# A two-layer DeltaNet and attention kernel: query heads' squared sums as four packed products, T joins spaced in the planner, and a new order in the scan's pool

## The chip, the cores and the metric

The kernel runs on one core of one Trainium2 chip. The metric is the device time of one execution in microseconds (us), taken as the median of several runs; lower is better. The core has five engines that matter here: TensorE (PE) multiplies matrices, VectorE (DVE), ScalarE (ACT) and GpSimd (POOL) work elementwise, and SyncE (SP) issues most of the DMA transfers. Each engine runs its instructions in the order in which they were written for it.

## The reference, cut to what matters

The input is 512 latent tokens and 256 context tokens of width 1024. Layer 0 is a bidirectional gated DeltaNet with 8 query/key heads and 16 value heads of width 128; layer 1 is attention; a final RMSNorm gives the output. Both layers read the tokens through an adaLN-modulated norm. The part around the change is this, from layer 0:

```python
p = u @ w_in                                           # 1024 -> q, k, v, z and gates
qkv = jax.nn.silu(centred_dwconv(p[..., :DN_CONV_DIM], conv_w))
q, k, v = jnp.split(qkv, [DN_KEY_DIM, 2 * DN_KEY_DIM], axis=-1)
q = jnp.repeat(l2_norm(q.reshape(b, l, DN_QK_HEADS, DN_HEAD_K)), rep, axis=2)
...
t_inv = lax.linalg.triangular_solve(eye + a, ...)      # per chunk of 64 tokens, per head
...
def step(s, xs):                                       # the scan over chunks
    v_new = u_i - jnp.einsum('bhcd,bhde->bhce', w_i, s)
    o = jnp.einsum('bhcd,bhde->bhce', qd_i, s) + jnp.einsum('bhcs,bhse->bhce', qk_i, v_new)
    s = s * gl_i[..., None, None] + jnp.einsum('bhcd,bhce->bhde', kd_i, v_new)
```

`l2_norm` needs, for each token and query head, the sum over 128 channels of the squared query. The kernel keeps queries unnormalised and applies this sum late, as a factor on the DeltaNet output (`rq`).

## The kernel before, in words

The core works through these stages: an opening (0 to about 44 us) that loads the tokens and forms the modulated, transposed input `uh` + `ul` (a high and a low part, so that fp32 accuracy comes from three fast products); the key heads (to about 134 us); the **planned stage** (134 to 541 us); the scan over chunks (541 to about 720 us); the output projection of layer 0 (to about 900 us); and layer 1.

In the planned stage PE forms 40 heads in the order of the string `order` (L898): 8 query (q), 16 value (v) and 16 gate (z) heads. One head is two `gemm_part` pieces (L919), the 512 latent columns and the 256 context columns, each of 24 products (8 slices of depth, three products each). Before a head's product its weights are split, by `w_high` on ACT and `w_low` on DVE or POOL (L914). After it come the convolution (`taps`), tanh and silu on ACT and DVE. A value head is then turned to token rows by PE (`head_turned`) and stored in DRAM.

A query head's squares (`head_squared`, ACT) lie with channels on the 128 partitions and the 768 tokens along the row. `head_summed` (L972) sums them over the partitions with PE: twelve products, one per chunk of 64 tokens, each with 64 columns of squares as the stationary operand and a column of ones as the moving one. `sums_copied` (L983) has ACT copy the 6 result columns into `rq`. One Newton series on DVE makes the roots of all of `rq` near the end of the stage (L1434).

Beside the heads, the stage makes the matrices T (the triangular solves) for six pairs of chunks, t = 0 to 5, in three solve pairs. Row loads and `decay` (L732, ACT), `m_prod` (L776, DVE) and turns build the input L of a pair, for which POOL runs a long chain of small column steps (`solve_steps`, L798). Then each t is **joined**: `j_turn` (L822, DVE), `j_first` (L830, PE, 64 products of 32 x 32), a negation on ACT, `j_second` (L854, PE, 64 products of 32 x 32), and copies on ACT into `Tt`, which `j_stored` (L851) writes to DRAM. Pair 2 (t = 4 and 5) is solved last. Each of the 64 products stands as two instructions in the trace with a weight load each, so that a join is 128 matmul records and as many weight loads.

The order of all this on the engines is written by a planner in the kernel's own Python. Every step is a `Piece` (L1037) with an engine, an assumed cost, a due time, the pieces that it comes after, and the buffers that it takes. `written_out` (L1110) repeatedly takes the piece that could start first by its model, and among equals the one that is due first, and so writes every engine's instruction order, SP's included. `margin` (L1055) adds a reserve of 3.0 us to PE pieces other than the `gemm_part` ones, which it knows by their cost.

The scan has 12 steps of 4 groups each. Step 0 needs no queries; its operands are loaded ahead by planned pieces (`first_matrices`, `first_values`). From step 1 on `load_step` (L1516) has SP issue the loads of keys (`ck`), values (`cv`), T (`cT`), QK (`cQK`), queries (`cq`) and turned keys (`ckt`). Their tiles come from the pool `ch` (L1450), which is laid over the planned stage's pool `tp`: both end at the same address, and inside a pool tiles lie in the order in which they are first asked for. A load therefore waits until the old tile under its target has been read for the last time. In the layout before, the query tile of step 1 lies over `U_5`, the last T's transposed solve, which `j_second` of t = 5 reads.

Of the kernel before, what the change touches and what calls it, by code (L numbers as in the profile page):

```python
# [17 lines left out]
P = 128  # L18
# [68 lines left out]
def backbone(tc, a, out):  # L87
# [147 lines left out]
    two = ap_.tile([P, 64], F32, tag="two", name="two", bufs=1)  # L235
    room = {}
# [8 lines left out]
    def opened():  # L245
# [10 lines left out]
        V.memset(ones, 1.0)  # L256
        V.memset(square, 1.0)
# [661 lines left out]
    def gemm_part(n, i):  # L919
        c, h = heads[n]  # L920
        wh, wl = split_w_[n]
        c0, m = COLS[i]
        ps = banks[n, i] = pa.tile([P, 512], F32, tag="g", name=f"g{m}_{c}{h}", bufs=4)
        for k in range(KT):
            for n_, (w, u) in enumerate(((wh, uh), (wh, ul), (wl, uh))):
                T.matmul(ps[:, :m], w[:, k], u[:, k, c0:c0 + m], start=k == 0 and n_ == 0, stop=k == KT - 1 and n_ == 2)  # L926
# [45 lines left out]
    def head_summed(n):  # L972
        ps = turns[n] = pa.tile([P, 512], F32, tag="tr", name=f"ss_q{heads[n][1]}")
        sq = sums.pop(n)
        for t in range(NT):
            for hf in range(2):
                c0 = t * P + hf * 64
                T.matmul(ps[hf * 64:hf * 64 + 64, t:t + 1], sq[:, c0:c0 + 64], ones, start=True, stop=True)
# [4 lines left out]
    def sums_copied(n):  # L983
        S.copy(rq[:, :, heads[n][1]], turns.pop(n)[:, 0:NT])
# [52 lines left out]
    class Piece:  # L1037
        def __init__(self, engine, cost, due, fn, *args, after=(), takes=(), holds=(), lands=0.0, since=0.0, slack=None, behind=(), port=0, sent=0.0, far=0.0):
# [3 lines left out]
            self.fn, self.end, self.takes = lambda: fn(*args), None, list(takes)  # L1042
            self.users = {x: [] for x in self.takes}
            for x, owner in holds:
                owner.users[x].append(self)
            pieces.append(self)

# [7 lines left out]
    def margin(x):  # L1055
# [4 lines left out]
        return MARGIN.get(x.engine, 0.0) if x.engine != "PE" else 0.0 if x.cost in (5.48, 2.96) else MARGIN["PE"]  # L1060
# [49 lines left out]
    def written_out():  # L1110

        left = list(pieces)
        while left:
            best = None
            for x in left:
# [12 lines left out]

    SLOT = 8.8
# [195 lines left out]
    for n, (c, h) in enumerate(heads):  # L1325
# [5 lines left out]
        g = []  # L1331
        for i in range(2):
            g.append(Piece("PE", (5.48, 2.96)[i], t0, gemm_part, n, i, after=[wh, wl] + ([last["g", n - 1]] if n and not i else g), takes=["g"], holds=[("wh", wh)], lands=0.2))
# [3 lines left out]
        if c != "z":  # L1337
            for i in range(2):
                ce = Piece("ACT", (0.65, 0.45)[i], e + (-2.9, 0.2)[i], centre, n, i, after=[g[i]] + a_[:1], takes=["acc"] if i == 0 else (), holds=[("g", g[i])] + ([("acc", a_[0])] if i else []), lands=0.1)
# [1245 lines left out]
```

## Time and profile before

| What | Value |
|---|---|
| Median of 3 runs | 1142.55 us (1142.25 to 1142.96) |
| The profiled execution | 1143.75 us, of which its span on the core is 1141.8 us |
| PE busy | 1107.7 us (97% of the span) |
| DVE, ACT, POOL busy | 790.3, 747.1, 602.1 us |
| TensorE clock granted, mean | 0.994 of full speed |
| Data moved by DMA | 208.69 MB, 183 GB/s on average |

The profile's rows give, for one profiled execution, an engine, a line of the kernel (L978 is line 978), the operation, the tile written and the tiles read, and times from the start of the span. Rows of the timeline begin with the start and the length; a bracket at the end tells the idle time of that engine ahead of the row and what ended it ("issue" is a gap for which no awaited event shows). Rows of a window give a stretch and each engine's busy time in it, then the granted clock, the share of the 16 DMA engines and the GB/s.

### The profile page before, as it was taken

What the parts mean: (1) busy time and instruction counts of PE and PEld (TensorE: products, weight loads), DVE (VectorE), ACT (ScalarE), POOL (GpSimd) and SP (SyncE); (2) the same over time, 40 slices, a digit from 0 to 9 for tenths busy, and PEclk for the clock granted to TensorE, in tenths of its full rate; (3) what the DMA queues carried; (4) which work ended last, traced back from release to release, by engine and by line L of the source; (5) the groups of instructions that cost most, each with busy time, mean ns of one, the idle gap of its engine ahead of it and who ended that gap; (6) DMA issues with size and microseconds to landing.
All of it is one profiled execution on the core that took longest, in us unless ns stands there. A gap on an engine that the chain in (4) does not pass through costs nothing. (4 is left out here: it accounts for less than half of the span.)

```text
span 1141.8 us, 27230 instructions
## 1 busy us (share of the span) xinstructions
PE 1107.7 (97%) x10511; PEld 904.8 (79%) x10511; DVE 790.3 (69%) x1628; ACT 747.1 (65%) x1990; POOL 602.1 (53%) x525
## 2 busy tenths in 40 slices
PE   5999999999999999998999999999999999999997
PEld 3677788888888888887666666788877889999886
DVE  4785666688899978783788878445555477667647
ACT  4554554477787888755689888875776356666731
POOL 0564111339999999950585598656654354130820
PEclk8999999999999999999999999999999999999999
DMA  9589744765838886766988984685854112101323
GB/s 367 187 297 329 254 151 124 226 175 163 238 123 246 262 250 201 200 209 185 283 236 255 279 241 129 206 216 173 246 162 139 37 56 75 38 19 57 111 74 92
DMA packets 117106, 208.69 MB, mean 183 GB/s; under 512 B 12113, under 2 KB 76786, under 8 KB 111730
## 3 DMA queue, kind: packets, MB, share of 16 engines
q1 hardware_dynamic: 97058, 195.32, 55.4%
q10 hardware_dynamic: 19920, 11.64, 3.5%
q8 instruction: 83, 1.36, 0.5%
q14 instruction: 45, 0.37, 0.1%
HBM read 166.16 MB, written 40.67 MB: 181 GB/s over the span
## 5 line engine op out<-in xcount | busy, mean ns | idle before, releaser
L1750 PE MATMUL po<-woh,y 128*128 128x512 f32 x384 | 129.3, 401 | 0.0
L1688 POOL TENSOR_TENSOR wol<-wo,woh 128x1024 fp32r<-128x1024 f32 x32 | 77.3, 2415 | 54.4 <-ACT woh L1681 52.6
L810 POOL TENSOR_TENSOR X<-X,tmp 128x62 f32<-128x62 f32 (+15 forms) x93 | 101.3, 1089 | 7.3
L1576 POOL TENSOR_TENSOR S<-S,glb 128x512 f32<-128x512 f32 x80 | 81.8, 1044 | 36.6 <-PE ks L1567 36.2
L809 POOL TENSOR_TENSOR tmp<-L,X 128x62 f32<-128x62 f32 (+15 forms) x93 | 89.1, 958 | 6.7
L926 PE MATMUL g_z<-ul,wh_z 128*128 128x512 f32 (+1 forms) x256 | 87.0, 340 | 3.0 <-issue 3.0
L926 PE MATMUL g_z<-uh,wh_z 128*128 128x512 f32 (+1 forms) x256 | 88.5, 346 | 0.2 <-issue 0.2
L926 PE MATMUL g_v<-uh,wh_v 128*128 128x512 f32 (+1 forms) x256 | 88.0, 344 | 0.0
L941 DVE SCALAR_TENSOR_TENSOR acc_v<-g_v,cwv,acc_v 128x510 f32<-128x510 f32 (+3 forms) x128 | 77.7, 614 | 14.5 <-ACT acc_v L933 11.0
L926 PE MATMUL g_z<-uh,wl_z 128*128 128x512 f32 (+1 forms) x256 | 86.6, 338 | 0.0
L926 PE MATMUL g_v<-ul,wh_v 128*128 128x512 f32 (+1 forms) x256 | 86.1, 336 | 0.0
L926 PE MATMUL g_v<-uh,wl_v 128*128 128x512 f32 (+1 forms) x256 | 86.1, 336 | 0.0
L1750 PEld LDWEIGHTS po<-woh,y 128*128 128x128 f32 x384 | 72.2, 188 | 15.6 <-issue 0.3
L1750 PE MATMUL po<-wol,y 128*128 128x512 f32 x192 | 75.5, 393 | 0.0
L1716 DVE SCALAR_TENSOR_TENSOR pt<-pt,og,z 128x128 f32<-128x128 f32 x96 | 34.4, 358 | 32.7 <-PE pt L1707 30.4
L1644 DVE TENSOR_TENSOR S<-su,S 128x512 f32<-128x512 f32 x80 | 51.5, 686 | 7.5 <-PE su L1630 5.9
L555 POOL TENSOR_TENSOR kt<-kt,kss 128x768 f32<-128x768 f32 x8 | 11.6, 1472 | 85.6 <-DVE kss L183 57.1
L926 PEld LDWEIGHTS g_z<-ul,wh_z 128*128 128x128 f32 x256 | 49.0, 191 | 8.4 <-issue 3.7
L1567 PE MATMUL ks<-S,ck 128*64 128x256 f32 x352 | 55.2, 392 | 0.0
L1570 DVE SCALAR_TENSOR_TENSOR r<-ks,negV,cv 128x128 f32<-128x128 f32 x176 | 52.3, 343 | 1.7 <-PE ks L1567 0.7
L1567 PE MATMUL ks<-S,cq 128*64 128x256 f32 x352 | 53.0, 379 | 0.3 <-DMA cq<-q_d 0.3
L926 PEld LDWEIGHTS g_z<-uh,wl_z 128*128 128x128 f32 x256 | 48.9, 191 | 5.3
(469 smaller groups left out, 3343.4 us busy)
## 6 DMA issues: line engine op xcount, KB each, us to landing
aw<-in_ada_late SPq DMA_DIRECT2D x16, 1024.0 KB, 6.9
wo<-in_dn_w_out SPq DMA_DIRECT2D x32, 512.0 KB, 3.7
cv<-v_d SPq DMA_DIRECT2D x22, 512.0 KB, 8.9
aw<-in_ada_first SPq DMA_DIRECT2D x8, 1024.0 KB, 10.4
w_z<-in_dn_w_in SPq DMA_DIRECT2D x16, 512.0 KB, 4.0
w_v<-in_dn_w_in SPq DMA_DIRECT2D x16, 512.0 KB, 4.5
v_d<-vt ACTq DMA_DIRECT2D x16, 384.0 KB, 4.0
cT<-t_d SPq DMA_DIRECT2D x12, 512.0 KB, 7.4
```

The lines of the kernel that those rows point to most:

```text
L555: G.tensor_tensor(kt, kt, bcast(r[:, h % 2 * NT:(h % 2 + 1) * NT], 2, P), ALU.mult)
L809: G.tensor_tensor(tv, bcast(L[:, :, j + 1:, j], 3, j + 1), bcast(X[:, :, j, 0:j + 1], 2, n), ALU.mult)
L810: G.tensor_tensor(X[:, :, j + 1:, 0:j + 1], X[:, :, j + 1:, 0:j + 1], tv, ALU.subtract)
L926: T.matmul(ps[:, :m], w[:, k], u[:, k, c0:c0 + m], start=k == 0 and n_ == 0, stop=k == KT - 1 and n_ == 2)
L941: V.scalar_tensor_tensor(acc[:, c0 + lo:c0 + hi], ps[:, lo + j - 2:hi + j - 2], cwv[:, j, ct:ct + 1], acc[:, c0 + lo:c0 + hi], ALU.mult, A ...
L1567: T.matmul(ks[r0:r0 + 64, w], kq[w][:, hh, r0:r0 + 64], St[hh][:, d], start=True, stop=True)
L1570: V.scalar_tensor_tensor(r[:, 2 * j + i], ks[:, 0, i], negV[:, visit, t, h:h + 1], v[:, h], ALU.mult, ALU.add)
L1576: G.tensor_tensor(St[hh], St[hh], bcast(g_, 3, P), ALU.mult)
L1644: V.tensor_tensor(St[hh], sj, St[hh], ALU.add)
L1688: G.tensor_tensor(wl, raws.pop(n), halves[n][0], ALU.subtract)
L1716: V.scalar_tensor_tensor(pj, pj, og, raw(z, off, [[st_, 2], [1, 64]]), ALU.mult, ALU.mult)
L1750: T.matmul(acc[nh], y[i][:, j, :], ww[k][:, nh * 512:(nh + 1) * 512], start=h == 0 and x == 0, stop=h == VH - 1 and x == 2)
```

## The change

It has five parts.

1. **Squared sums.** `head_summed` now keeps a small selector as stationary operand (`pick`, zeros with one column of ones, of which 32 columns are taken so that the ones stand in column h) and streams the squares: four products of 192 tokens each, one to each group of 32 columns of the array, so that row h of each group of the result holds head h's sums. DVE collects the 8 heads into `qrows` (128 x 192). After the last head, `sums_turned` turns them with six products against the identity, and `sums_kept` copies them to `rq` with two ACT copies.
2. **Joins apart.** The planner remembers the end of the last `j_first` or `j_second` and lets the next one count as startable only 4.0 us after it (`SPACED`).
3. **Halved heads.** For the last three heads (n = 37, 38, 39, all z) each `gemm_part` becomes two pieces of 12 products, between which the planner may put other PE work.
4. **Three due times.** `m_prod` of t = 5 is due 373 us later, one of the query-side `decay` pieces of t = 3 is due 22 us later, and `w_low` of head 10 is due 23 us earlier.
5. **Scan pool.** The tiles of `ch` are asked for once in a fixed order ahead of the scan, and the two `r` buffers become two tags, the second at the end. All tiles between them lie 2 KB per partition lower than before; the query tile of step 1 no longer touches `U_5`.

```diff
+    pick = ap_.tile([P, 64], F32, tag="pick", name="pick", bufs=1)
+    qrows = ap_.tile([P, 192], F32, tag="qrows", name="qrows", bufs=1)
...
+        V.memset(pick, 0.0)
+        V.memset(pick[:, 32:33], 1.0)
...
-    def gemm_part(n, i):
+    def gemm_part(n, i, half=None):
...
-        ps = banks[n, i] = pa.tile([P, 512], F32, tag="g", name=f"g{m}_{c}{h}", bufs=4)
-        for k in range(KT):
+        if half != 1:
+            banks[n, i] = pa.tile([P, 512], F32, tag="g", name=f"g{m}_{c}{h}", bufs=4)
+        ps = banks[n, i]
+        for k in range(KT) if half is None else range(half * 4, half * 4 + 4):
...
     def head_summed(n):
...
-        for t in range(NT):
-            for hf in range(2):
-                c0 = t * P + hf * 64
-                T.matmul(ps[hf * 64:hf * 64 + 64, t:t + 1], sq[:, c0:c0 + 64], ones, start=True, stop=True)
+        for g in range(4):
+            T.matmul(ps[32 * g:32 * g + 32, 0:192], pick[:, 32 - h:64 - h], raw(sq, g // 2 * 384 + g % 2 * 64, [[P, 3], [1, 64]]), start=True, stop=True, tile_position=(0, 32 * g))
...
     def sums_copied(n):
-        S.copy(rq[:, :, heads[n][1]], turns.pop(n)[:, 0:NT])
+        ps = turns.pop(n)[:, 0:192]
+        if heads[n][1] == 0:
+            V.tensor_copy(qrows, ps)
+        else:
+            V.tensor_tensor(qrows, ps, qrows, ALU.add)
+
+    def sums_turned():
+        ps = turns["q"] = pa.tile([P, 4, P], F32, tag="tr", name="ss_t")
+        for j in range(3):
+            for hf in range(2):
+                T.matmul(ps[hf * 64:hf * 64 + 64, j], qrows[:, j * 64:j * 64 + 64], ident, start=True, stop=True)
+
+    def sums_kept():
+        ps = turns.pop("q")
+        for hf in range(2):
+            rows = slice(hf * 64, hf * 64 + 64)
+            S.copy(rq[rows].rearrange("p (a j) h -> p a j h", j=3), raw(ps[rows], 32 * hf, [[64, 2], [P, 3], [1, QH]]))
...
+            self.due += moved.get(name + (seen[name],), 0)
+            self.dense = fn in (j_first, j_second)
...
+    moved, seen = {('m_prod', (5, 0), 1): 373, ('decay', (3, 0, 12, 16), 2): 22, ('w_low', (10,), 1): -23}, {}
...
-                key = (max(r, free[x.engine]), x.due)
+                key = (max(r, free[x.engine], dense + SPACED if x.dense else 0.0), x.due)
...
+            if x.engine == "PE":
+                start = max(ready_at(x), free["PE"])
             passed(x, start)
+            dense = x.end if x.dense else dense
...
+    HALVED, SPACED = 37, 4.0
...
+            one = Piece("PE", (2.74, 1.48)[i], t0, gemm_part, n, i, 0, after=before, takes=["g"], holds=[("wh", wh)], lands=0.2)
+            gb.append(one)
+            g.append(Piece("PE", (2.74, 1.48)[i], t0, gemm_part, n, i, 1, after=[one], holds=[("wh", wh), ("g", one)], lands=0.2))
...
-        for i in range(2):
-            ch.tile([P, 4, P], F32, tag="r", name=f"r_{i}", bufs=2)
+        ch.tile([P, 4, P], F32, tag="r0", name="r_0", bufs=1)
         St = [ch.tile([P, 2, 2, P], F32, tag=f"S{hh}", name=f"S{hh}", bufs=1) for hh in range(QH)]
+        for tag, shape, n in (("vn", [P, 4, P], 2), ("vd", [P, 4, P], 2), ("T", [P, VH, 64], 1), ("v", [P, VH, P], 1), ("QK", [P, VH, 64], 1),
+                              ("kt", [P, QH, P], 1), ("kq0", [P, QH, P], 1), ("kq1", [P, QH, P], 2), ("o", [P, 4, P], 2), ("r1", [P, 4, P], 1)):
+            for i in range(n):
+                ch.tile(shape, F32, tag=tag, name=f"{tag}_first{i}", bufs=n)
...
-            r = ch.tile([P, 4, P], F32, tag="r", name=f"r{x}", bufs=2)
+            r = ch.tile([P, 4, P], F32, tag=f"r{x % 2}", name=f"r{x}", bufs=1)
```

More of the change, by code (lines that the diff above doesn't have):

```diff
@@ L972, in head_summed @@
     def head_summed(n):
[L973 removed]
+        h = heads[n][1]
+        ps = turns[n] = pa.tile([P, 512], F32, tag="tr", name=f"ss_q{h}")
         sq = sums.pop(n)
[L975 to L978 removed]
+        for g in range(4):
+            T.matmul(ps[32 * g:32 * g + 32, 0:192], pick[:, 32 - h:64 - h], raw(sq, g // 2 * 384 + g % 2 * 64, [[P, 3], [1, 64]]), start=True, stop=True, tile_position=(0, 32 * g))
     def head_turned(n):
@@ L1110, in written_out @@
     def written_out():
-        left = list(pieces)
+        left, dense = list(pieces), 0.0
         while left:
@@ L1330, in backbone @@
         wl = Piece("POOL" if G_ else "DVE", 2.38 if G_ else 1.22, t0 - 5, w_low, n, G if G_ else V, port=1, after=[wh], holds=[("w", w)], lands=0.1)
-        g = []
+        g, gb = [], []
         for i in range(2):
-            g.append(Piece("PE", (5.48, 2.96)[i], t0, gemm_part, n, i, after=[wh, wl] + ([last["g", n - 1]] if n and not i else g), takes=["g"], holds=[("wh", wh)], lands=0.2))
+            before = [wh, wl] + ([last["g", n - 1]] if n and not i else g)
+            if n < HALVED:
+                g.append(Piece("PE", (5.48, 2.96)[i], t0, gemm_part, n, i, after=before, takes=["g"], holds=[("wh", wh)], lands=0.2))
+                gb.append(g[i])
+                continue
+            one = Piece("PE", (2.74, 1.48)[i], t0, gemm_part, n, i, 0, after=before, takes=["g"], holds=[("wh", wh)], lands=0.2)
+            gb.append(one)
+            g.append(Piece("PE", (2.74, 1.48)[i], t0, gemm_part, n, i, 1, after=[one], holds=[("wh", wh), ("g", one)], lands=0.2))
         last["g", n] = g[1]
@@ L1338, in backbone @@
             for i in range(2):
-                ce = Piece("ACT", (0.65, 0.45)[i], e + (-2.9, 0.2)[i], centre, n, i, after=[g[i]] + a_[:1], takes=["acc"] if i == 0 else (), holds=[("g", g[i])] + ([("acc", a_[0])] if i else []), lands=0.1)
+                ce = Piece("ACT", (0.65, 0.45)[i], e + (-2.9, 0.2)[i], centre, n, i, after=[g[i]] + a_[:1], takes=["acc"] if i == 0 else (), holds=[("g", gb[i])] + ([("acc", a_[0])] if i else []), lands=0.1)
                 a_.append(ce)
-                tp_ = Piece("DVE", (3.2, 1.75)[i], e + (0.5, 2.4)[i], taps, n, i, after=[ce], holds=[("g", g[i]), ("acc", a_[0])], lands=0.1)
+                tp_ = Piece("DVE", (3.2, 1.75)[i], e + (0.5, 2.4)[i], taps, n, i, after=[ce], holds=[("g", gb[i]), ("acc", a_[0])], lands=0.1)
                 a_.append(tp_)
@@ L1433, in backbone @@
             kept(("QK", t, v), Piece("SP", 1.3, due + 14, q_store, t, v, after=[pr], holds=[("df", r[v])], sent=2.2))
-    Piece("DVE", 2.4, T0 + N * SLOT - 5, lambda: [f_() for f_ in rsqrt_steps(rq.rearrange("p t h -> p (t h)"), 1.0)], after=[last["rq", h] for h in range(QH)], since=T0 + 376.0)
+    st_ = Piece("PE", 0.7, T0 + 170, sums_turned, after=[last["rq", QH - 1]], takes=["tr"], lands=0.1)
+    sk_ = Piece("ACT", 0.5, T0 + 180, sums_kept, after=[st_], holds=[("tr", st_)], lands=0.1)
+    Piece("DVE", 2.4, T0 + N * SLOT - 5, lambda: [f_() for f_ in rsqrt_steps(rq.rearrange("p t h -> p (t h)"), 1.0)], after=[sk_], since=T0 + 376.0)
     at = T0 + N * SLOT - 60
```

12 lines of the change are left out of this document (7 added, 5 removed).

## The prediction, on record before the run

> **What bounds the kernel now.** I read the page first, then the busy time by stretches, then who waited for whom inside the planned stage, then the timeline around every gap that this left. All times are of one profiled execution: 1143.75 us, its span 1141.8 us, so 1.95 us lie around the span. It lies 1.2 us above the median of the runs, 1142.55 us; I take the gain from the trace and subtract it from the median. About 0.2% (2.3 us) is what a measurement of this kernel can tell from no change.
>
> ```profile
> span 1141.8 us, 27230 instructions
> ...
> q8 instruction: 83, 1.36, 0.5%
> ```
> ```profile
> 134.00:541.00 407.00, 401.90 (x4436) 350.26 (x4436) 314.17 (x459) 279.58 (x684) 253.29 (x224) 1.00 0.66 194
> 525.00:530.00 5.00, 3.77 (x107) 3.15 (x108) 0.00 (x0) 4.37 (x9) 0.00 (x0) 0.73 0.67 252
> ```
> ```profile
> PE g_z L926 <- issue: 3.2, 3, 2.2
> PE pp L837 <- issue: 1.9, 1, 1.9
> ```
>
> The second fence has, after the stretch and its length, the busy time of PE, weight loads, DVE, ACT and POOL. In the planned stage PE works 401.90 of 407 us, while DVE has 93 us to spare. The third is the whole list of PE's waits there: 5.1 us in four gaps, and none of them for another engine. So this stage ends when PE has issued its work, and an instruction taken off PE shortens the stage by its time on PE. The gaps lie at its end, in the timeline of PE:
>
> ```profile
> 522.77 1.29 PE L861 MATMUL pw<-pn,U 32*32 32x32 f32 x128
> 523.90 0.44 PE L837 MATMUL pp<-U,mo 32*32 32x32 f32 x28
> 526.23 1.05 PE L837 MATMUL pp<-U,mo 32*32 32x32 f32 x100 [1.89 <-issue]
> 527.22 0.70 PE L926 MATMUL g_z<-uh,wh_z 128*128 128x512 f32 x1
> ...
> 530.70 0.43 PE L926 MATMUL g_z<-uh,wl_z 128*128 128x512 f32 x1
> 530.97 0.40 PE L926 MATMUL g_z<-uh,wh_z 128*128 128x512 f32 x1
> 531.20 0.40 PE L926 MATMUL g_z<-ul,wh_z 128*128 128x512 f32 x1
> ...
> 534.50 1.29 PE L861 MATMUL pw<-pn,U 32*32 32x32 f32 x128
> ...
> 538.62 0.39 PE L926 MATMUL g_z<-ul,wh_z 128*128 128x256 f32 x1 [2.17 <-issue]
> ...
> 541.21 0.67 PE L1593 MATMUL pr_all<-cv,cT 64*64 64x128 f32 x16
> ```
>
> The second join of t = 4 and the first of t = 5 stand back to back: 256 products and as many weight loads in some 2.3 us. PE stops 28 products into the second, in the middle of a run of like instructions, with no event awaited. I read this as instructions that had not arrived: the page's q8 row shows that the instruction stream itself comes by DMA, 83 packets for 1.36 MB. Behind the gap, eight products of 512 columns take 3.48 us (527.22 to 530.70) where the usual spacing is 0.23 us (530.97 to 531.20), 1.64 us too much, and the granted clock of 525 to 530 us is 0.73. So this collision costs 1.89 + 1.64 = 3.53 us. The later gap of 2.17 us follows a single join (534.50) and no slow products follow it.
>
> **Squared sums.** The old form:
>
> ```profile
> 214.59 1.57 PE L978 MATMUL ss_q<-ones,sq_q 128*64 128x1 f32 x48
> 216.09 1.10 PE L761 MATMUL G<-kq_0m 128*32 128x64 f32 x64
> ```
> ```profile
> 130.71 1.92 PE L316 MATMUL pa<-aw,sc 128*32 128x512 f32 x16
> 132.57 0.50 PE L500 MATMUL g_k<-uh,wh_k 128*128 128x512 f32 x1
> ```
>
> Two heads' sums hold PE for 1.50 us (214.59 to 216.09), so one head costs 0.75 us. The new form is four column groups at 192 columns, eight records a head. The trace has no such shape, but has it on both sides: eight records of four groups at 512 columns take 0.93 us (half of 130.71 to 132.57), at 64 columns 0.14 us (an eighth of the 1.10 us of G). On the line between, 192 columns give 0.37 us. Bounds are 0.14 and 0.93; I take 0.40, near the line, with a little for the change of shape. Eight heads save 8 x 0.35 = 2.8 us; at the ends 4.9 saved or 1.4 lost.
>
> The new turn of the rows, six products or twelve records of 128 columns with 64 stationary ones:
>
> ```profile
> 548.37 0.60 PE L1567 MATMUL ks<-S,ck 128*64 128x256 f32 x4
> 548.80 0.60 PE L1567 MATMUL ks<-S,cq 128*64 128x256 f32 x4
> ```
>
> Four records of 256 columns over the two halves take 0.43 us there; twelve of half the length come to 0.65 us, twice that if the halves don't overlap. I take 0.75 us. Net on PE: 2.8 - 0.75 = **2.05 us** saved.
>
> Elsewhere eight short ACT copies and one wait go, and DVE gets eight passes over 192 columns:
>
> ```profile
> L960 DVE SCALAR_TENSOR_TENSOR sil_v<-g_v,acc_v x32: 386/531/711, 275.7 to 512.3; 128x512 f32<-128x512 f32 x16, 128x256 f32<-128x256 f32 x16
> ```
>
> The smallest of those, 256 columns, is 0.386 us, so at most 3.1 us more on DVE, inside its 93 idle us: nothing. If PE had to wait for DVE there, all of it would count. The two memsets stand in the opening, while DVE waits for its first loads: nothing. The two ACT copies and the single turn lie ahead of the roots, which are due at the stage's end: nothing.
>
> **Joins apart, halved heads.** The two parts act together. With 4.0 us of model time between dense pieces, `j_first` of t = 5 can't follow `j_second` of t = 4 directly; the half heads (about 2.75 or 1.5 us) are the filling, and let the first join of t = 4 start a half head earlier. They add no product. The collision of 3.53 us should go. The gap of 2.17 us I leave in: it came behind a single join, with DMA at its densest, and that remains. Gain **3.5 us**; bounds: none (every gap returns elsewhere) and 5.7 us (the third goes too).
>
> The Trainium skill speaks against this part: its page "Runtime: NRT & Kernel Launch", section "Instruction fetch mechanics", says that instructions are streamed in blocks of 16 KiB and that crossing a block is mostly hidden. The trace agrees on the size (1.36 MB in 83 packets) but not on the hiding, given a gap inside a run of 128. By the rule the gap would have another cause and the spacing gain nothing: 2.05 us in all.
>
> The page "TensorE: Matmul & The Clock Gate", section "What's actually happening", puts the drop to half clock behind an idle window of about 3.4 us. Here the slow products follow 1.89 us of idleness, so the row goes against the length that it asks for. By the rule the 1.64 us would stay and the sum be 3.9 us.
>
> **Start of the scan.** If PE comes 5.6 us earlier, the scan's first loads must too.
>
> ```profile
> 526.80 0.33 SPq L852 DMA_DIRECT2D t_d<-Tt  x1
> 527.53 0.32 SPq L1533 DMA_DIRECT2D ck<-k_d  x1
> ...
> 535.86 0.32 SPq L1540 DMA_DIRECT2D cq<-q_d  x1
> ```
> ```profile
> SPq L1540 <- PE pw L861: 3.6, 1, 3.6
> ```
> ```profile
> 547.89 0.65 PE L1567 MATMUL ks<-S,cq 128*64 128x256 f32 x4 [0.28 <-DMA cq<-q_d]
> ```
>
> SP stands behind the store of t = 4's T (526.80), then issues keys, values, T and QK of step 1; the query load waits 3.6 us for `j_second` of t = 5, because its tile lies over that product's operand. It lands only at 547.89, 12 us after its issue, and PE already waits 0.28 us for it. There is no slack here now. The new pool order takes the query tile off that operand: 3.6 us. The store of T(4) comes earlier by the 2.05 us of the sums and a half head (up to 2.7 us), about 4.5 us in all. Together up to 8 us against the 5.6 needed, but the same DMA engines carry all of it, so I charge **0.4 us** (bounds 0 and 3.6, the wait as it was).
>
> **Due times.** `w_low` 23 us earlier and the `decay` 22 us later only trade places on DVE and ACT: nothing, inside the idle time above. `m_prod` of t = 5 feeds the last solve pair:
>
> ```profile
> 343.51 1.92 POOL L796 TENSOR_TENSOR L<-L,bball 128x1024 f32<-128x1024 f32 x1 [0.31 <-DVE L L791]
> ```
> ```profile
> 423.40 1.82 POOL L802 MEMSET X<- 128x2048 f32 x1
> ```
> ```profile
> 515.17 2.22 DVE L828 STREAM_TRANSPOSE U<-X 128x1024 f32<-128x1024 f32 x1
> ```
>
> Its result is ready at 345.4 and pair 2 begins at 423.40, when POOL is done with pair 1: 78 us of cover. A later due time makes it last among what DVE could start at the same moment, no more. Nothing, unless the 78 us are used up.
>
> **Sum.** 2.05 + 3.5 - 0.4 = 5.2 us: from 1142.55 to **1137.4 us**. Everything behind the scan's start keeps its work and shifts.
>
> **Rivals.**
> - *Both gaps go* (0.14). With the joins spread from t = 4 on, the last one may meet arrived instructions. For it: the 2.17 us gap is the same kind. Against: DMA stays dense. Another 2.2 us: 1135.2 us.
> - *The gap only moves* (0.22). Instructions arrive late wherever a join meets dense DMA, however the joins are spaced. For it: the 2.17 us gap behind a lone join. Against: the earlier lone joins left at most the small rest of the four gaps, 1.0 us. Gain 2.05 us: 1140.5 us, on the border of what can be told. The rule of "Runtime: NRT & Kernel Launch" above, in the Trainium skill, would give the same time.
> - *The last pair comes late* (0.09; the slower case). The last U now ends at 517.4 us (515.17 + 2.22). Four joins with 4.0 us between them, the first at about 515, end near 531; PE's other work would last to 541.0 - 5.6 = 535.4. So 4.6 us of lateness are covered and beyond that PE waits one for one. If `m_prod` of t = 5 sinks so far that pair 2 starts after 423.40, this is used up; slower by over 2.3 us needs 12 us of lateness, at 15 us the time is 1137.4 + 15 - 4.6 = 1147.8 us. Against: DVE's 93 idle us, in which the piece would be taken, and 78 us of cover.
> - *The change doesn't do what it says* is in the second of these: the spacing is counted in model time, and the chip may run the two joins closer.
>
> **How the numbers follow.** The forecast has 0.53, its own range 1135 to 1140. Faster by over 0.2%: 0.53, 0.14 and half of the 0.22, less a little for a plan that turns out otherwise, 0.74. Within: the other half and some of the forecast's upper end, 0.15. Slower: 0.11, the late pair and 0.02 for several new gaps. The range goes from 1133.0 (both gaps, and the better bound of the squares, 2.1 us more) to 1143.0 (nothing gained, and the 0.4 us lost); the late pair and a part of the flat cases above it are what it leaves out.
>
> **What would show it.** Right: `ss_q` with 64 records in all and about 0.4 us a head; no gap inside a `pp` or `pw` run, no clock below 1 at 515 to 535; the scan's first product near 535.6; the query load issued right behind QK. Wrong: a gap of 1 to 2 us behind another join; PE waiting for `U` or `pn` in the last 30 us (the late pair); a wait for `cq` or `cv` of over 1 us.

## The result, and the profile after

The change makes the kernel slower. The median after is 1148.04 us (1146.53 to 1151.04, 7 runs), before 1143.47 us on the same chip (1142.25 to 1145.68, 7 runs); the ratio is 1.0047, with a 95% interval of 1.0033 to 1.006. I had forecast 1137.4 us, and 1148.04 lies above the range. Most runs of one kernel lie within some 3 us of its median here, so the verdicts below rest on ratios of many runs, and single profiles serve only for what they show of a mechanism. The profiled execution took 1150.16 us; from its page:

```profile
span 1148.4 us, 26997 instructions
...
q8 instruction: 82, 1.34, 0.5%
```

The work on PE went as forecast. The squared sums and their turn, in PE's timeline (start, length, the operation, partitions and columns, count):

```profile
214.60 0.86 PE L983 MATMUL ss_q<-sq_q,pick 128*32 128x192 f32 x16
215.39 0.39 PE L932 MATMUL g_q<-uh,wh_q 128*128 128x256 f32 x1
...
372.80 0.83 PE L999 MATMUL ss_t<-ident,qrows 128*64 128x128 f32 x12
373.56 0.38 PE L932 MATMUL g_z<-uh,wh_z 128*128 128x256 f32 x1
```

Two heads hold PE for 0.79 us (I said 0.40 a head), the turn for 0.76 us (0.75). The pair of joins no longer collides either: in the window of 525 to 530 us the granted clock was 0.73 before and is 1.00 now.

```profile
525.00:530.00 5.00, 5.00 (x34) 4.58 (x33) 0.00 (x0) 4.50 (x9) 0.00 (x0) 1.00 0.54 210
```

But the whole list of PE's waits in the planned stage is not empty:

```profile
PE g_q L932 <- DVE sil_z L964: 2.0, 1, 2.0
PE g_z L932 <- issue: 1.9, 2, 1.0
PE g_v L932 <- issue: 0.8, 1, 0.8
```

4.7 us in four gaps, where before had 5.1 us; the first is new, a wait for VectorE. Products at half clock follow it, eight steps of 0.43 us in place of 0.23 us, 1.6 us more:

```profile
250.57 0.50 PE L932 MATMUL g_q<-uh,wh_q 128*128 128x512 f32 x1 [1.99 <-DVE sil_z L964]
...
251.60 0.55 PE L932 MATMUL g_q<-ul,wh_q 128*128 128x512 f32 x1
251.96 0.63 PE L932 MATMUL g_q<-uh,wl_q 128*128 128x512 f32 x1
...
254.94 0.47 PE L932 MATMUL g_q<-uh,wh_q 128*128 128x512 f32 x1
```

So the scan's first product comes at 538.93 us, 2.3 us sooner than the 541.21 of before, not 5.6. And then the scan's start loses more than all of it:

```profile
538.93 0.67 PE L1637 MATMUL pr_all<-cv,cT 64*64 64x128 f32 x16
...
541.28 0.67 PE L1666 MATMUL pr_all<-vn,cQK 64*64 64x128 f32 x16 [1.25 <-DVE vn L1639]
...
545.22 0.32 PE L1666 MATMUL pq_all<-vn,cQK 64*64 64x128 f32 x1 [1.45 <-issue]
...
552.44 1.12 PE L1611 MATMUL ks<-S,cq 128*64 128x256 f32 x4 [5.42 <-DMA cq<-q_d]
553.35 1.07 PE L1611 MATMUL ks<-S,ck 128*64 128x256 f32 x4
...
555.20 0.77 PE L1637 MATMUL pq_all<-cv,cT 64*64 64x128 f32 x16
```

PE waits 5.42 us for step 1's query tile (0.28 before), and the three groups behind the wait take 2.76 us (552.44 to 555.20) where they took 1.44 us (547.89 to 549.33). Two smaller losses stand in the same rows, and the kernel before has neither at this place: 1.25 us of waiting for VectorE's `vn`, and a gap of 1.45 us for which no event shows. The query load is issued at 538.34 on SP's queue, where before it went out at 535.86:

```profile
526.43 0.32 SPq L856 DMA_DIRECT2D t_d<-Tt  x1
533.42 1.12 SPq L1031 DMA_DIRECT2D cv<-v_d  x2
534.65 0.53 SPq L1577 DMA_DIRECT2D ck<-k_d  x1
535.23 1.08 SPq L1031 DMA_DIRECT2D cv<-v_d  x2
536.36 0.59 SPq L1581 DMA_DIRECT2D cT<-t_d  x1
537.98 0.33 SPq L1582 DMA_DIRECT2D cQK<-qk_d  x1
538.34 0.65 SPq L1584 DMA_DIRECT2D cq<-q_d  x1
```

```profile
SPq L1031 <- DMA v_d<-vt: 6.5, 1, 6.5
```

The store of T(4) (`t_d`) went out at 526.43, almost as before (526.80). Behind it SP stands 6.5 us in `first_values`, the load of value heads 12 to 15 for the scan's step 0, which needs value head 15 to have been stored. In the kernel before SP stood 5.4 us for the same store, but ahead of the store of T(4) and only until 523.57 us, so that no load behind it was late. In ACT's timeline that head's copy now comes behind the copies of the second join of t = 4; before, copy and store came ahead of them, at 519.79 and 520.68 us:

```profile
524.05 2.35 ACT L872 COPY Tt<-pw 32x512 f32<-32x512 f32 x4 [0.63 <-PE pw L865]
526.43 0.86 ACT L1012 COPY vt<-tr_v 128x512 f32<-128x512 f32 x2
527.32 0.37 ACTq L1013 DMA_DIRECT2D v_d<-vt  x1
```

The planner had put head 15's turn behind that join. This was the first theory: SP's wait for head 15's store makes step 1's loads some 7 us late. The rival: the DMA engines are full here (a share of 0.96 to 1.00 from 535 to 550 us), so the order and the bytes decide, not the time of issue.

### The profile page after: what moved, and what is told of

It is laid out like the page before. It is cut to its first block, busy times and chain, and to the rows that moved or that the text cites. A ratio compares the mean times of both kernels' runs of the same rounds, so it can differ in the third digit from the quotient of the medians.

```text
span 1148.4 us, 26997 instructions
## 1 busy us (share of the span) xinstructions
PE 1108.0 (96%) x10395; PEld 901.3 (78%) x10395; DVE 785.1 (68%) x1638; ACT 747.6 (65%) x1984; POOL 603.0 (53%) x525
## 5 line engine op out<-in xcount | busy, mean ns | idle before, releaser
L932 PEld LDWEIGHTS g_z<-uh,wh_z 128*128 128x128 f32 x256 | 48.5, 189 | 7.3 <-issue 2.2
```

## The experiments

In each, "stage" is the time from the first `g_q` product to the first product of the scan, and "scan on" from there to the end of the span, both in the profiled execution. The kernel before has 396.05 and 600.59 us, the changed one 393.75 and 609.47 us. One profile's stage is uncertain by several us: the changed kernel, e1, e2 and e5 write the same instructions in the same order there and took 393.75, 395.96, 390.81 and 391.31 us, and the kernel before and e10, again alike there, took 396.05 and 392.11 us.

| Kernel | Ratio to before, 95% | Stage | Scan on | Wait for `cq` |
|---|---|---|---|---|
| changed | 1.0047 (1.0033 to 1.006) | 393.75 | 609.47 | 5.4 |
| e1 other heads read | 1.002 (1.0004 to 1.0036) | 395.96 | 603.31 | 1.1 |
| e2 = changed, again | 1.0052 (1.0035 to 1.007) | 390.81 | 609.64 | 6.4 |
| e3 head 15 first | 1.0024 (1.0008 to 1.0039) | 396.88 | 604.51 | none |
| e4 joins only | 0.9999 (0.9986 to 1.0012) | 389.86 | 608.18 | 5.1 |
| e5 changed, query second | 0.9996 (0.9979 to 1.0014) | 391.31 | 605.96 | none |
| e6 joins, query second | 0.9979 (0.9964 to 0.9994) | 393.25 | 601.19 | none |
| e7 changed, old sums | 1.0007 (0.9993 to 1.0021) | 390.29 | 606.11 | 5.5 |
| e8 before, 32 products more | 1.0099 (1.0077 to 1.0122) | 391.25 | 603.24 | none |
| e9 e7, query second | 0.996 (0.9947 to 0.9973) | 390.58 | 601.98 | none |
| e10 before, query second | 1.0001 (0.999 to 1.0011) | 392.11 | 605.47 | none |
| e11 e5, one due time back | 0.999 (0.9975 to 1.0004) | 392.46 | 605.20 | none |
| e12 e4, joins unspaced | 0.9999 (0.9986 to 1.0013) | 393.50 | 602.36 | 2.5 |
| e13 new sums, old order | 0.9962 (0.9948 to 0.9977) | 390.66 | 602.65 | none |
| e14 old sums, new order | 1.0022 (1.0008 to 1.0036) | 395.32 | 601.69 | none |

### Does SP's wait for head 15's store cost it? (e1, e2, e3)

```diff
+            s0 = 4 if h0 == 12 else h0          # e1, values_loaded
-            dma(v[...], v_d[..., h0:h1])
+            dma(v[...], v_d[..., s0:s0 + h1 - h0])
```

> The changed kernel, but the second half of the scan's first value loads reads value heads 4 to 8, stored long before, in place of 12 to 16 (so heads 12 to 15 of the first tile get wrong values; nothing else differs, the planned order included). SyncE then has nothing to wait for at that load. Theory 1 (the loss is that wait: step 1's loads stand behind it on SyncE, which waits 6.5 us for value head 15's store): the load issues at once after the store of T(4), step 1's loads start some 6 to 7 us earlier, the wait of 5.4 us at the first ks product of the queries goes, with it the slow products behind it; time about 1141.5 us, 6 to 7 us under the changed kernel, ratio to the kernel before 0.998. Theory 2 (the DMA engines are saturated around 520 to 550 us, so an earlier issue only lets the transfers compete earlier): at most 3 us gained, ratio 1.002 to 1.005.

Ratio 1.002; PE's wait fell from 5.4 to 1.1 us. SP went on to the keys at 530.23 at once, but stood again at step 1's own values, which need head 15's store as well:

```profile
528.24 1.89 SPq L1032 DMA_DIRECT2D cv<-v_d  x2
530.23 1.69 SPq L1578 DMA_DIRECT2D ck<-k_d  x1
535.36 1.09 SPq L1032 DMA_DIRECT2D cv<-v_d  x2
...
538.16 0.39 SPq L1585 DMA_DIRECT2D cq<-q_d  x1
```

The query tile was issued as late as in the changed kernel (538.16 to 538.34) and yet landed 3 us sooner (549.4 to 552.4): what stood ahead of it had been moved earlier. That speaks for the rival, and asked for a test of the order itself.

```diff
-    for h0, h1 in ((0, 12), (12, VH)):          # e2
+    for h0, h1 in ((0, 12),):
...
                 dma(kq[1], q_d[t])
+                first_values(12, VH)            # load_step, s == 1
```

> The changed kernel with the full computation, but the load of value heads 12 to 15 for the scan's first tile is issued behind step 1's query tile instead of ahead of step 1's loads. Theory 1: as with the other heads, the ks wait goes; the value load itself now comes at about 535 us, after head 15's store has landed, and is needed at 541; about 1141.5 us, ratio 0.998. If the first pr product waits for this load instead (a wait moved, not removed), 2 to 4 us stay and the ratio is 1.001 to 1.003. Theory 2: ratio 1.002 to 1.005.

A miss of mine: behind the planned stage SP's order is made by the framework's scheduler, and it set this load ahead of step 1's loads again, where it was. SP's rows show the same order as in the changed kernel. So this is a second set of runs of the changed kernel, 1.0052; its stage was 2.9 us shorter than in the first profile and its wait for the query tile 1 us longer.

```diff
-            tu = Piece("PE", 0.6, t0 - 20, head_turned, n, ...     # e3
+            tu = Piece("PE", 0.6, t0 - 20 if n < 36 else -40, head_turned, n, ...
```

> The changed kernel with one due time changed: the turn of value head 15 stands ahead of the second join of t = 4, as in the kernel before, so its copy and store no longer stand behind that join's copies. The value load stays where it is on SyncE. Theory 1: head 15's store issues some 5 us earlier and SyncE waits some 5 us less; ratio 0.998 to 1.000. Theory 2: ratio 1.002 to 1.005. If head 15's store is late because of the DMA queue and not because of the turn's place, its landing moves by under 2 us and the ratio stays at 1.003 or above.

Ratio 1.0024, half of the loss; the wait for `cq` is gone, since SP issued values, keys and T 3 to 6 us sooner. The query load itself went out later than in the changed kernel (540.17 against 538.34) and yet took 5.7 us from issue to landing in place of 14.1. So the place of head 15's store is part of the cause (some 0.25%, good to about 0.2%), but not all of it: this kernel is still slower than before. In its profile the scan lost time at another place, by a gap of 2.31 us at 698.70 us with a granted clock of 0.57 over the next 4 us.

### The joins alone (e4), and without the spacing (e12)

e4 is the kernel before with the planner's lines for halved heads and spaced joins, nothing else:

```diff
+    HALVED, SPACED = 37, 4.0
...
-                key = (max(r, free[x.engine]), x.due)
+                key = (max(r, free[x.engine], dense + SPACED if x.dense else 0.0), x.due)
```

> The kernel before with only the joins kept apart and the z heads halved from head 37 on (old squared sums, old due times, old tiles). Theory 1 with theory 3 (gaps come at blocks of 256 instructions behind dense joins, so a spacing only moves them): the planned stage gains under 2 us. In this kernel head 15's turn stands behind the second join of t = 4 as well, so the scan start loses its 5 us: ratio 1.003 to 1.006, as the whole change. Rival (the gaps go with the spacing, as I predicted, and the loss comes from the squared sums or the shifted due times): the stage gains 3.5 us and the ratio is 0.996 to 0.998.

Ratio 0.9999: neither expectation. I was wrong that head 15's turn slides in this kernel: it stays ahead of the join, and SP doesn't wait for it. In its profile the stage is 6.2 us shorter than in the profile of before (396.05 to 389.86), more than I had forecast; two profiles can't settle that size, since the plan of before took 392.11 us in e10. PE's timeline at its end, with one short gap:

```profile
520.41 1.29 PE L861 MATMUL pw<-pn,U 32*32 32x32 f32 x128
526.00 1.29 PE L837 MATMUL pp<-U,mo 32*32 32x32 f32 x128
531.59 1.22 PE L861 MATMUL pw<-pn,U 32*32 32x32 f32 x121
533.61 0.26 PE L861 MATMUL pw<-pn,U 32*32 32x32 f32 x7 [0.80 <-issue]
535.42 0.67 PE L1612 MATMUL pr_all<-cv,cT 64*64 64x128 f32 x16
```

All of it is lost in the scan's first steps, in a wait for a query tile that lands at 547.72 us, just when it landed before (547.89):

```profile
547.72 1.12 PE L1586 MATMUL ks<-S,cq 128*64 128x256 f32 x4 [5.06 <-DMA cq<-q_d]
```

SP's rows tell why. The load went out at 540.90 us, 5 us later than before (535.86), because SP stood ahead of it for the store of a gate head:

```profile
540.90 0.32 SPq L1559 DMA_DIRECT2D cq<-q_d  x1
```
```profile
SPq L1559 <- DMA z_d<-sil_z: 7.7, 1, 7.7
```

That store was itself 10.6 us on its way (5.7 in the kernel before), and the load then took 6.8 us. In both kernels the DMA engines are fully busy (a share of 0.95 to 1.02 in every window of 5 us) from 530 us to 545 us, and T(5)'s store of 1 MB goes among the loads. So PE came 5.8 us earlier and met a tile that had not moved: in the kernel before it spent 12.0 us on its way, here SP waited for a store that was longer on its way. I read that longer way as the work of the full engines; no run tests it apart.

e12 takes the spacing out again, so that the two joins stand back to back:

```diff
-    HALVED, SPACED = 37, 4.0
+    HALVED, SPACED = 37, 0.0
```

> The kernel before with the z heads halved from head 37 on, but no spacing: the second join of t = 4 and the first of t = 5 still stand back to back. Theory 3 (a gap stands where a block of 256 instructions has not arrived, and two joins back to back use up a block in 1.2 us): a gap of 1.5 to 2.2 us near the pair of joins stays, and the planned stage ends between 537.5 and 541 us, against 535.5 with the spacing and 541.2 before. Rival (the halved heads alone bring the gain): the stage ends at or under 536 us with no gap over 1 us. In both cases the scan's start takes most of it back: ratio 0.998 to 1.002.

Ratio 0.9999 (0.9986 to 1.0013), stage 393.5 us, and the collision is back at its old size, with slow products behind it:

```profile
522.62 1.29 PE L861 MATMUL pw<-pn,U 32*32 32x32 f32 x128
523.76 0.54 PE L837 MATMUL pp<-U,mo 32*32 32x32 f32 x40
526.21 1.40 PE L837 MATMUL pp<-U,mo 32*32 32x32 f32 x88 [1.91 <-issue]
```

So it is the spacing that removes the collision, and the halving alone doesn't. The rival of this run falls. The query load is late in the same way as in e4: SP stood 9.8 us for the gate head's store, and PE waited 2.5 us.

### The place of the query tile (e5, e6, e10)

```diff
             dma(kq[0], k_d[t])
-            if s > 1:
-                dma(kq[1], q_d[t])
+            dma(kq[1], q_d[t])
             values_loaded(t, v)
             dma(Tt, t_d[t, :, visit])
             dma(QK, qk_d[t, :, visit])
-            if s == 1:
-                dma(kq[1], q_d[t])
```

> The changed kernel with step 1's query tile loaded directly behind its key tile, ahead of the values, T and QK tiles, instead of behind them. Theory now (the first runs showed the DMA engines busy at a share of 1.0 from about 530 us until the query tile lands, 16 to 20 us later, whatever SyncE waited for): at the scan's start the DMA bandwidth is the bound, and the query tile is late because 3 MB stand ahead of it that are needed later. Then the ks wait of 5.4 to 6.4 us goes, with the slow products behind it; the next wait is for step 1's values or T, some 4 to 6 us later, and costs 0 to 3 us. Ratio to the kernel before 1.000 to 1.002, against 1.0047 for the changed kernel. Rival (SyncE's wait for head 15's store is the cost, and the order behind it doesn't matter): the wait moves to the values or the T tile at its full size, ratio 1.004 to 1.006.

Ratio 0.9996, 0.5% better than the changed kernel, by three moved lines. The `ks` products run through, 10 us sooner than in the changed kernel; the query load takes 6.2 us from issue to landing in place of 14.1, and neither the values nor T become a new wait:

```profile
541.83 0.65 PE L1608 MATMUL ks<-S,ck 128*64 128x256 f32 x4
542.31 0.60 PE L1608 MATMUL ks<-S,cq 128*64 128x256 f32 x4
542.75 0.60 PE L1608 MATMUL ks<-S,ck 128*64 128x256 f32 x4
```

The order of the loads is what counts, not only their start. SP still waited for head 15's store here (values issued at 529.63, 7 us behind the store of T(4)), and it cost PE nothing. The scan as a whole was not yet as short as before (605.96 us to the end, against 600.59): in this profile the wait for `vn` stays with 1.43 us, and gaps of 0.5 to 1.0 us are strewn over its later steps.

e6 is e4 with the shifted tiles of the pool and these lines.

> The kernel before with the joins kept apart and the halved z heads, the shifted tiles, and step 1's query tile loaded directly behind its key tile; old squared sums, old due times. In the joins alone (ratio 0.9999) the planned stage ended 5.7 us sooner and the ks products then waited 5.1 us for the query tile. Theory (DMA bound at the scan's start, its order decides): that wait goes and 3 to 5 us of the stage's gain stay; ratio 0.9955 to 0.998, faster than both kernels. Rival (the bytes decide, not their order): the wait moves to the values or T of step 1, ratio 0.999 to 1.001.

Ratio 0.9979 (0.9964 to 0.9994): faster than both kernels, as the theory had it, though at the upper end of what I expected; in this profile a gap of 1.53 us came back inside the last join. Two things differ from e4, the place of the load and the tile under it, and no run takes them apart: the load went out at 528.68 us, and SP's wait for the gate head's store (7.3 us) now stood ahead of QK, where it cost PE nothing. The order alone is tested by e5 against the changed kernel and by e9 against e7.

e10 is e6 without the halved heads and the spacing.

> The kernel before with nothing but the shifted tiles and step 1's query tile loaded second: joins and sums as before. There TensorE came to the ks products 0.28 us before the query tile. Theory: with nothing waiting for that tile, its earlier load is worth 0.3 us at most; ratio 0.999 to 1.0005. So the faster kernel needs both, a stage that ends sooner and the tile early. Rival (the early query tile is the whole gain of the faster kernel): ratio 0.997 to 0.998.

Ratio 1.0001. With the joins unspaced the early tile brings nothing. The gain needs both: a stage that ends sooner and a tile that is there. This rests on the ratios; the one profile of e10 has a short stage (no slow products behind its collision) and loses the time again in the scan, by a gap of 2.17 us at 544.00 us with a clock of 0.50 behind it. The step from e10 to e6, 0.22% (2.5 us, good to about 0.2%), is the cleanest price of the spaced joins that these runs give.

### The sums and the planner's order (e7, e9, e11, e13, e14)

e7 puts the old sums back into the changed kernel, plan and all; its core:

```diff
-        for g in range(4):
-            T.matmul(ps[32 * g:32 * g + 32, 0:192], pick[:, 32 - h:64 - h], ...)
+        for t in range(NT):
+            for hf in range(2):
+                T.matmul(ps[hf * 64:hf * 64 + 64, t:t + 1], sq[:, c0:c0 + 64], ones, ...)
```

> The changed kernel with the old squared sums: joins apart, shifted due times and shifted tiles stay. Its planned order differs: head 15's turn stands behind the first join of t = 5, later still than in the changed kernel, and the wait of PE for a z silu near 250 us should be gone, as that came with the new order around the sums. Theory (what decides is when head 15's store lets SyncE go on): the query tile lands later than in the changed kernel (after 552 us) and the ratio is 1.005 or above, in spite of 3.6 us less lost near 250 us. Rival (the new sums and the order they bring are the loss): ratio 0.999 to 1.002.

Ratio 1.0007: the theory behind this expectation falls, the rival holds. Head 15's turn is later still in the plan, but the whole stage runs ahead and the query tile lands at 546.48, not after 552. Without the new sums the kernel is 0.4% better, although I had them down as a gain of 2.05 us.

e9 is e7 with the three lines of e5.

> The changed kernel with the old squared sums and step 1's query tile loaded second. With the old sums alone the stage ended at 534.6 us, the ks products then waited 5.5 us for the query tile, and eight of them ran at half clock behind it; ratio 1.0007. Theory (the order of the loads decides at the scan's start, since the DMA engines are full from 527 us on): the wait and the slow products go, 5 to 7 us; another 1 to 3 us may come back as a wait for step 1's values or T; ratio 0.995 to 0.998, at or below the joins with the query tile second (0.9979). Rival (bytes, not order): 1.000 to 1.001.

Ratio 0.996 (0.9947 to 0.9973), together with e13 the fastest kernel of the study: 1138.7 us against 1142.94. The wait and the half clock behind it went, and no other wait for a transfer came in their place. Its kernel differs from that of e6 by the three due times alone; the ratio is 0.19% lower, which is on the border of what can be told.

e11 is e5 without the shifted due time of head 10's weight half:

```diff
-    moved, seen = {..., ('w_low', (10,), 1): -23}, {}
+    moved, seen = {...}, {}
```

> The changed kernel with step 1's query tile second and without one of the three shifted due times, that of the low half of the weights of head 10 (23 us earlier in the changed kernel). Theory: the 2.0 us that TensorE waits for a z silu near 250 us in every run with the new sums come from VectorE's new order there (the squares' rows, that weight half and the G masks ahead of the silu), and the shifted weight half is what tips it: without it the wait is under 0.7 us. Rival (the new sums' passes on VectorE alone make it): it stays at 2.0 us. The time is not the point here, since the last pairs' pieces move too; 0.997 to 1.002.

Ratio 0.999 (0.9975 to 1.0004). PE's wait near 250 us stayed, 2.11 us, now for `wl_q` itself: the shifted weight half only chooses which piece is late. With that due time and without it VectorE stands over 2 us for the products G of pair 1, which PE does at 227.45 in the kernel before and behind 48 more head products, at 234.52, in the changed one; VectorE's row in the changed kernel is

```profile
235.25 0.29 DVE L773 TENSOR_TENSOR Gx<-G,masks 128x128 f32<-128x128 f32 x1 [2.38 <-PE G L765]
```

I read this as PE waiting for VectorE at 250 us because VectorE had waited for PE at 235 us; in the kernel before, VectorE's longest wait for G there is 0.2 us. That left the question whether the sums do this or the order around them. The last two runs are the missing corners: e13 emits the new sums at the places where the planner has the old ones (plan, costs and engines of the old pieces kept), e14 the reverse (on e5, with `sums_turned` and `sums_kept` empty).

```diff
-    Piece("DVE", 2.4, ..., lambda: [f_() for f_ in rsqrt_steps(...)], after=[last["rq", h] ...     # e13, on e9
+    Piece("DVE", 2.4, ..., lambda: [sums_turned(), sums_kept()] + [f_() for f_ in rsqrt_steps(...)], after=...
```

> The new squared sums put into the places that the old sums have in the kernel with the old sums and the query tile second (ratio 0.9960): the planner still counts the old pieces, so its order of all other work is that of the old sums; the eight products, VectorE's passes, the turn and the copies are those of the new sums. Two by two with the two kernels measured: old sums in the old order 0.9960, new sums in the new order 0.9996. Theory (the new sums' products save the 1.9 us that I forecast, and the order that the planner makes around them loses it): 0.994 to 0.996. Rival (the new sums themselves cost, by VectorE's passes that wait in order for the products): 0.998 to 1.000.

> The other corner: the old products and copies of the squared sums in the places that the new sums have in the changed kernel with the query tile second (ratio 0.9996); the planner's order is that of the new sums. Theory (the order loses): the wait of 2.0 us for a z silu near 250 us stays, the old products come on top; 1.000 to 1.002. Rival (the new sums themselves cost): 0.996 to 0.998, and the wait near 250 us is gone or under 0.7 us.

| All with the query tile second | Old order | New order |
|---|---|---|
| Old sums | 0.9960 (0.9947 to 0.9973) | 1.0022 (1.0008 to 1.0036) |
| New sums | 0.9962 (0.9948 to 0.9977) | 0.9996 (0.9979 to 1.0014) |

"Old order" is the order that the planner writes with the old pieces and all else of the change in place; it isn't that of the kernel before. The four kernels ran on three chips, each against the kernel before on the same chip. Down a column or along a row, each difference is good to about 0.2%. The order costs 0.34% with the new sums and 0.62% with the old; the sums change nothing that can be told in the old order and save 0.26%, barely clear, in the new. The 2.05 us that I forecast for the sums are 0.18%, which neither excludes. Both new corners lie at the upper end of what the theory gave or just over it (0.996 and 1.002), and well off the rival's ranges. So the order loses, not the sums. PE's waits in the stage say the same, first of e13, then of e14:

```profile
PE g_z L932 <- issue: 1.3, 1, 1.3
PE g_v L932 <- DVE sil_z L964: 1.0, 1, 1.0
```

```profile
PE pw L865 <- issue: 2.4, 1, 2.4
PE g_q L932 <- DVE sil_z L964: 2.0, 1, 2.0
```

The 2.0 us near 250 us come with the order even when the sums are the old ones, and go with it.

### Where the gaps without a releaser stand (e8)

```diff
         T.transpose(rr["pv"][:, 0:64], rr["vr"], ident[0:64, 0:64])
+        for _ in range(32):
+            T.matmul(rr["pv"][:, 100:101], rr["vr"], rr["vr"][:, 0:1], start=True, stop=True)
```

> The kernel before with 32 tiny products more, in the opening where TensorE is idle; nothing else. They shift the place of every later instruction of TensorE within the blocks of 256 at whose ends I found the gaps without a releaser. Theory 3 (a gap stands where a new block of instructions has not arrived): the gap inside the first join of t = 5 (behind product 28 of 128) moves to another place in the instruction stream, by half a block or less, so into the second join of t = 4 or further into the first of t = 5; it keeps 1 to 2 us, and the gap of 2.17 us at 538.6 moves by as many instructions. Rival (the gap belongs to the two joins back to back, at the place where a queue in front of the array runs dry): it stays behind product 28. Time within 0.3% of the kernel before either way.

The 32 products are 64 records and 64 weight loads, 128 instructions. The gap moved by exactly 64 records, from behind the 28th of the join's 128 to behind the 92nd:

```profile
536.10 1.29 PE L863 MATMUL pw<-pn,U 32*32 32x32 f32 x128
537.28 1.01 PE L839 MATMUL pp<-U,mo 32*32 32x32 f32 x92
540.37 0.52 PE L839 MATMUL pp<-U,mo 32*32 32x32 f32 x36 [2.07 <-issue]
```

From the gap at 526.23 us of the kernel before to the next at 538.62, the window of its profile holds 256 records and 256 loads:

```profile
526.22:538.61 12.39, 10.22 (x256) 8.23 (x256) 0.69 (x1) 6.32 (x11) 0.00 (x0) 0.86 0.94 257
```

The later gap moved too: it has 2.90 us and stands in the scan's first products, at 555.91. All profiles together say the same. Counting every row of PE, weight loads and issues included, in order of time, each of the 56 gaps of over 0.4 us without an awaited event, from 134 to 720 us of all 16 profiles, stands 193 or 194 rows past a multiple of 256. Such a place comes 926 times in these stretches, and the gaps go with how long PE took for the block ahead of it: the gap is there at 23 of 71 places where that was under 4 us, at 33 of 471 from 4 to 8 us, and at none of the 384 of 8 us or more. So these gaps stand at the ends of blocks of 256 instructions, in the scan as well as behind joins. I read them as a block that PE needs before it has arrived, and the two joins back to back, 512 instructions in 2.3 us, use such blocks up fastest. Theory 3 holds, its rival falls. Of the time I was wrong: the ratio is 1.0099, because PE was not idle for the dummies. They took 13.75 us of the opening (0.21 us a record), and the first `g_q` product came 14.35 us later. The stage itself was 391.25 us.

## Why the prediction was wrong, point by point

- **Squared sums: right on PE, wrong beside it.** 0.40 us a head and 0.76 us for the turn, 2.08 us saved where I said 2.05. What failed is the step that called everything else of this part "nothing": I took the planner's order as given. New costs and engines for eight pieces made it write another order for the whole rest of the stage, and that order cost 0.34% to 0.62% (3.9 to 7.1 us of 1143), by e13 and e14. Parts of it are named: the 2.0 us for VectorE near 250 us, with 1.6 us of half clock in some executions, the wait of 1.25 us for `vn`, and head 15's store behind the join (some 0.25%, e3). How the rest divides is open.
- **Joins apart: right in the mechanism, the size a little lower.** The collision went, and by e12 the spacing does it. What that is worth shows once the query tile is early: 2.5 us by e10 and e6, good to some 2 us, against my 3.5. The 6.2 us between the profiles of e4 and before lie above my bound of 5.7, and part of them is the spread of single executions. In the changed kernel itself the gain doesn't show, since the other order put new gaps into the stage (4.7 us and 1.6 us of half clock, against 5.1 and 1.64 before). The gap that "only moves" (0.22) was half right: the places are block ends, e8 moved one, and in the changed kernel one of 1.45 us stands in the scan's start; but a spaced join leaves less of it.
- **Start of the scan: this is the step that failed most.** I wrote that SP's loads would come up to 8 us sooner and charged 0.4 us, with 3.6 at the worst. Measured: 5.42 us of wait, 0.28 before, and 1.3 us of slow products; a wait for `cq` of over 1 us was among my signs of being wrong. The new pool order did what I said, the query load went out right behind QK. Two things were wrong. The loads don't only stand behind the store of T(4), but behind `first_values` too, whose own wait I had not asked about (5.4 us before, 6.5 now, and now behind that store). And from its issue the tile took 14.1 us to land, with the DMA engines full. My sentence "there is no slack here now" was right, and "the same DMA engines carry all of it" should have been the price: here all that PE gained was lost at that tile, by transfers that take 10 to 14 us among the others and by SP's waits for such stores (e4), until the tile's place in the order of loads was changed (e5, 0.5%).
- **Due times: nothing on its own** by e11, for the weight half (0.06%, good to about 0.2%). The other two were not tested singly; the three together, from e6 to e9, may save up to 0.4% or nothing. I had asked what each moved piece itself may cost, not what the plan does with it.
- **The last pair comes late** was my slower case, with its point at PE waiting for U or `pn`. No run shows such a wait. The slower outcome came by another road, which I had no rival for.
- **A slip in the sums.** The times by the two rules, 2.05 and 3.9 us of gain, leave out the 0.4 us that I charged for the scan's start; with it they are 1.65 and 3.5 us. Nothing above hangs on this.

On the two rules weighed in the prediction. The Trainium skill's page "Runtime: NRT & Kernel Launch", section "Instruction fetch mechanics", has blocks of 16 KiB, 256 instructions, and their crossing mostly hidden: the count between gaps (256 + 256) and e8's shift agree with the block, and "mostly" agrees with 56 gaps at 926 ends, but where a block was used up in under 4 us the crossing was not hidden at 23 of 71. The Trainium skill's page "TensorE: Matmul & The Clock Gate", section "What's actually happening", calls the activity window free-running, so that the point of transition depends on where in the window the products fall. The variation agrees: the same wait of 2.0 us near 250 us was followed by a clock of 0.64 to 0.66 over 4 us in the changed kernel, e1 and e3, and of 1.00 in e2, e5 and e14. The length for which the prediction cites that page doesn't: gaps of 1.53 to 2.90 us were followed by half clock too.

## What to carry to other kernels

Before an engine's time is counted as gain, look for the next point where it meets a transfer, and ask what sets that transfer's landing: here, with the DMA engines full, a stage that ended 5.8 us sooner brought nothing (e4), and a load moved up in the row brought 0.5% (e5, e9). In a kernel whose order is written by a planner, a cheaper piece is a new order: keep the old order and swap only the instructions (as e13 does) to tell what the piece is worth, then judge the order by itself. And follow an in-order queue through every entry ahead of the one that matters, with the wait of each.

## What the runs showed of the hardware that was not expected

- After a gap of about 2 us TensorE may or may not fall to half clock. Beside the 2.0 us near 250 us (three of six runs, above): after 1.89 us (before) and 2.63 us (e1) the clock over the next 4 us was 0.64 and 0.59; after 2.17 us (before) and 2.07 us (e8) it was 1.00; after 5 to 6 us (e2, e4, e7) it was 0.50 or 0.51. Over the stage and the scan of all 16 profiles the clock fell behind none of the 33 gaps of 0.75 to 1.5 us, behind 10 of the 22 of 1.5 to 2.5 us, and behind all 7 longer ones.
- The same planned stage (the changed kernel and e2) has its gaps at the same places but of other lengths: 0.98 and 1.54 us near 349 us, 0.80 us and none near 405 us. The places belong to the program, the lengths to the execution.
- The moving columns alone don't tell a product's price: 64 records with one moving column and a stationary operand of 64 x 128 held PE for 13.75 us in e8 (0.21 us each), while the old sums' 48 records, also with one moving column and with 128 x 64, take 1.50 us (0.03 us each). What makes the difference is not shown.
